# A list scheduler with new priorities: the same instructions of a decoder trunk, issued in another order

## The chip, the cores and the metric

The kernel runs on one core of one Trainium2 chip. The metric is device time in microseconds (us): the median of three runs of the kernel before is 1182.84 (1181.1 to 1184.08). Engines are named as in the profile: PE multiplies matrices, DVE, ACT and POOL do elementwise work, SP issues most DMAs.

## The reference, cut to what matters

Two decoder layers on one sequence of 512 rows with 1024 columns, all in float32:

```python
for l in range(DEPTH):                       # DEPTH = 2
    h = x @ w_in[l]
    q, k, v, u = jnp.split(h, splits, axis=-1)
    attn_out = diff_attention(q, k, v, lam, lam_init, subln_g[l], cos, sin)   # 4 heads, causal, rotary
    ssm_out = s5_ssm(u, ssm_lam_re[l], ...)  # 32 groups, complex diagonal scan, then GELU and GLU
    mix = jnp.concatenate([attn_out, ssm_out], axis=-1) @ w_out[l]
    x = layer_norm(ALPHA * x + mix, ln1_g[l], ln1_b[l])
    ff = jnp.square(jax.nn.relu(x @ w_ff1[l])) @ w_ff2[l]
    x = layer_norm(ALPHA * x + ff, ln2_g[l], ln2_b[l])
```

w_in maps 1024 to 2048 columns, w_ff1 1024 to 4096, w_ff2 back to 1024.

## The kernel before, in words

Each float32 product is made of three products of rounded parts. A weight block of 128x1024 comes by a DMA of SP's queue into a buffer `raw`; ACT rounds it to `whi`; the rest `wlo` = raw - whi is made by one of three routes, chosen by letters in the table `PLAN`: "V" a subtraction on DVE, "P" the same on POOL, "A" a negated rounding on ACT followed by an accumulating DMA from POOL's queue (`wsplit`, line 542, and `gsplit`). PE then runs hi by hi, hi by lo and lo by hi (`mm3`). There are five `raw` buffers and four each of `whi` and `wlo`.

A layer has these stages. The back stage makes q, k, v and u by projections, four heads of attention (`attn_u`, one unit for each head and block of 128 queries), the S5 part in four quarters (parameters `ssm_pars` and `ssm_outp`, then `ssm_a`, `ssm_b`, `ssm_c`) and the gated unit `glu`. Then come w_out with the first norm, and the feed-forward stage in eight chunks: in each, `ffone` makes four products of w_ff1, and `fftwo` seven products of sums of blocks (m1 to m7) of w_ff2. The last chunk (`ffend`) ends with the second norm. Three quarters of the second layer's S5 parameters are made while the first layer's feed-forward runs, stored to DRAM (`keep`, 12 tiles of 256 KB), and loaded again later.

Nothing is issued as it is written. `Rec.add` (line 215) records every operation with its tiles. `Rec.schedule` gives each a rank (the longest chain behind it), and `Rec.run` (line 350) goes through time with a duration for each operation (`Rec.cost`, line 261), takes the ready operation of highest rank plus offset on each engine, and so makes one fixed order for each engine. The offsets are set around parts of the program by `early(n, pe)`, `n` for all engines but PE and `pe` for PE. A tile could take a buffer only in the order in which tiles were written (`turn` at line 405). Where the plan expects PE to wait, `fill` puts in products of a zero tile `wz` (columns 256, into a bank that is overwritten later); they are allowed only between the exponentials of an attention unit and its product with v (`rec.spare`, in `attn_u`). 18 such products stand at the program's start.

All engine work is recorded under line 492 of the kernel before, where it is issued, and so the profile's groups are told apart by tile names: `ps_acc`, `ps_sc`, `ps_s` are banks of PSUM.

Of the kernel before, what the change touches and what calls it, by code (L numbers as in the profile page):

```python
# [19 lines left out]
P = 128  # L20
# [29 lines left out]
    "lo": ["AVAVVAAAAAAVAAAAAAAA", "AAAAAAAAAAAAAAAVAAVP"],  # L50
    "eng": {"rope": ["VVV", "VVV"], "tab": ["VVVVVV", "VVVVVV"], "cg": ["VVVV", "VVVV"], "ch": ["VVVV", "VVVV"], "sa": ["VV", "VP"], "sb": ["VVVVVV", "VVVVVV"]},
# [6 lines left out]
    "s5o": "p1 p0 o0 a0 b0 p2 a1 c0 o1 b1 a2 c1 b2 p3 a3 o2 c2 o3 b3 c3",  # L58
# [14 lines left out]
    "po": -6000,  # L73
    "m3": 4,
    "gap": [250, 500],
# [34 lines left out]
class View:  # L110
# [37 lines left out]

    def cells(self):
        m = 0  # L150
        for c in np.unique(self.idx // self.t.cell):
            m |= 1 << int(c)
# [12 lines left out]
class Op:  # L165
    __slots__ = ("eng", "name", "a", "k", "succ", "nd", "dur", "tail", "tiles", "new", "rank", "t0", "t1", "ready", "n",
                 "soft", "move", "table", "off", "port", "rows")


class Rec:  # L170
    def __init__(self, nc):
        self.real = {"PE": nc.tensor, "DVE": nc.vector, "ACT": nc.scalar, "POOL": nc.gpsimd, "DMA": nc.sync}
        self.ops, self.tiles, self.spares = [], {}, {}
        self.off = (0, 0)
# [86 lines left out]
    def cost(self, op, views):  # L261
# [88 lines left out]
    def run(self):  # L350
# [4 lines left out]
        turn, live, rel, wait = {}, {}, {}, {}  # L355
        for key, ts in self.tiles.items():
            turn[key], rel[key], wait[key] = 0, [0.0] * ts[0].bufs, []
            for i, t in enumerate(t for t in ts if t.first is not None):
                t.n = i
        left = {}  # L360
# [14 lines left out]
        for op, (a, b) in self.spares.items():  # L375
            for o in a:
                opens.setdefault(o, []).append(op)
            closes[b] = op
            op.nd, op.ready = len(a), 0.0
        while len(order) < len(self.ops):  # L380
# [23 lines left out]
            for v in op.new:  # L404
                if turn[v.key] != v.n or not rel[v.key]:
# [10 lines left out]
            for v in op.new:  # L416
                heapq.heappop(rel[v.key])
                turn[v.key] += 1
# [16 lines left out]
            if op in closes and closes[op] in live:  # L435
                live.remove(closes[op])
# [42 lines left out]
            for key in woken:  # L479
                for o in wait[key]:  # L480
                    heapq.heappush(future[o.eng], (max(o.ready, rel[key][0] if rel[key] else t), o.n, o))
# [14 lines left out]
def trunk(ctx, tc, x, xt, w_qk, w_v, w_u, w_glu, w_out, w_ff1, w_ff2, lam_qk, subln, lam_s, bc_s, d_s, glu_b,  # L496
# [40 lines left out]


# [89 lines left out]
    for i in range(PLAN["warm"]):  # L628
        PE.matmul(wb_[:, 0:256], wz[:, 0:P], wz, start=True, stop=True)
# [418 lines left out]
    def attn_u(l, h, b):  # L1048
# [13 lines left out]
        for m in range(2):  # L1062
            PE.matmul(scm[m][:, :n], qT[m][:, b * P:n], kT[m][:, :n], start=True, stop=False)
# [19 lines left out]
        for j in range(b + 1):  # L1083
            op = PE.matmul(o[:, 0:P], ats[:, j, :], vj(j), start=(j == 0), stop=(j == b))
            if j == 0:
                rec.spare(ex, op, o[:, 0:256], wz[:, 0:P], wz, start=True, stop=True)
# [201 lines left out]
    for l in range(L):  # L1288
# [6 lines left out]
        for h in range(NH):  # L1295
            t0 = PLAN["att"][l][h]
            for b in range(NB):
                side[min(t0 + b, len(back))].append(lambda h=h, b=b: attn_u(l, h, b))
            side[min(max(t0 + NB, PROJ * (h > 1)), len(back))].append(lambda h=h: attn_fin(l, h))
        s5 = []  # L1300
        made = [l > 0 and PLAN["store"][qd] in "sx" for qd in range(4)]
        def S(f, qd):
            return lambda: f(l, qd)
# [22 lines left out]
        for i in range(len(back) + 1):  # L1326
            if i < len(back):
                p0 = 0
                back[i]()
                d = 0  # L1330
            else:
                d = 0
            for fs, off, pe in ((side[i], PLAN["ao"][l], PLAN["ap"][l]), (s5side[i], PLAN["so"][l], PLAN["sp"][l])):
                with early(off, pe):
                    for f in fs:
                        f()

# [306 lines left out]
```

## Time and profile before

| what | us |
|---|---|
| median of three runs | 1182.84 |
| the profiled execution | 1184.34 |
| its span, first to last instruction | 1182.6 |
| PE busy in the span | 1124.1 (95%) |
| DVE busy | 883.4 (75%) |
| ACT busy | 643.7 (54%) |
| POOL busy | 382.9 (32%) |
| mean granted clock of PE | 0.987 of full speed |

The first layer runs from 0 to about 600 us, its back stage to about 200; the second layer's back stage lies between about 600 and 800. An instruction's duration on PE includes the way through the array; how fast PE goes is read from the distance of two starts. A clock of 1.00 is 2.4 GHz, 0.50 is 1.2 GHz.

### The profile page before, as it was taken

To read this page: it belongs to the slowest core of one execution; us is meant where nothing else is said; L and a number is where in the kernel's file an instruction comes from. 1 tells how busy PE (TensorE), PEld (TensorE's weight loads), DVE (VectorE), ACT (ScalarE), POOL (GpSimd) and SP (SyncE) were. 2 spreads that over 40 slices of the span, in tenths; PEclk is the share of its full clock that TensorE was granted. 3 is DMA by queue.
4 is the path that set the end of the run, shared out by engine and by line. 5 is a ranking of instruction groups with operands and counts; after the bars stand their busy time and mean duration, and the time that the engine had idled before them with its cause. 6 is when DMAs were issued, how large, how long until landed. Compare 5 with 4: busy or idle time off the path is not lost.

```text
span 1182.6 us, 16083 instructions
## 1 busy us (share of the span) xinstructions
PE 1124.1 (95%) x5755; PEld 933.8 (79%) x5755; DVE 883.4 (75%) x1517; ACT 643.7 (54%) x1214; POOL 382.9 (32%) x250
## 2 busy tenths in 40 slices
PE   8798989999999999999998989999999999999997
PEld 6678867788888888878888878777988787777775
DVE  7898997876867866878873978767587657656668
ACT  6677778425554555455256777763454445354450
POOL 1010111234454443553221211123344435445341
PEclk9899999999999999999999999999999999999999
DMA  7532624442653654565683663532553554464341
GB/s 242 150 80 72 150 74 134 149 128 73 175 144 93 168 149 109 168 166 133 204 212 89 174 174 94 176 108 85 155 153 98 165 144 114 133 161 117 114 125 72
DMA packets 52689, 160.41 MB, mean 136 GB/s; under 512 B 7041, under 2 KB 7297, under 8 KB 52609
## 3 DMA queue, kind: packets, MB, share of 16 engines
q1 hardware_dynamic: 42240, 121.63, 31.6%
q0 software_dynamic: 10368, 37.75, 17.1%
q8 instruction: 45, 0.74, 0.3%
q14 instruction: 36, 0.29, 0.1%
HBM read 110.07 MB, written 7.34 MB: 99 GB/s over the span
## 4 chain that ended last, share of the span: by engine, by line
PE 63%; ACT 12%; issue 7%; DMA 7%; DVE 6%; POOL 4%; SPq 1%; DVEq 0%; ACTq 0%; POOLq 0%
PE ps_acc L492 36%; PE ps_sc L492 15%; PE ps_s L492 12%; DMA wlo<-raw 6%; POOL wlo L492 4%; ACT whi L492 3%; ACT u L492 3%; DVE slot L492 2%; ACT xq L492 1%; ACT at L492 1%; DVE xq L492 1%; ACT wlo L492 1%; DMA raw<-in_w_qk_dram 1%; ACT slot L492 1%; SPq L492 1%
## 5 line engine op out<-in xcount | busy, mean ns | idle before, releaser
L492 POOL TENSOR_TENSOR wlo<-raw,whi 128x1024 fp32r<-128x1024 f32 x110 | 276.8, 2519 | 355.6 <-ACT whi L492 355.6
L492 ACT CAST whi<-raw 128x1024 fp32r<-128x1024 f32 x222 | 230.0, 1049 | 271.4 <-PE ps_acc L492 112.9
L492 PE MATMUL ps_acc<-xTh,whi 128*128 128x512 f32 (+1 forms) x712 | 269.3, 382 | 18.1 <-ACT whi L492 13.8
L492 PE MATMUL ps_acc<-xTh,wlo 128*128 128x512 f32 (+1 forms) x712 | 270.1, 383 | 6.7 <-DMA wlo<-raw 6.7
L492 PE MATMUL ps_acc<-xTl,whi 128*128 128x512 f32 (+1 forms) x712 | 268.3, 381 | 1.1 <-DVE xTl L492 1.0
L492 PE MATMUL ps_sc<-whi,slot 128*128 128x512 f32 x784 | 257.8, 393 | 1.6
L492 PEld LDWEIGHTS ps_sc<-whi,slot 128*128 128x128 f32 x784 | 147.1, 188 | 37.3 <-DVE xq L492 3.2
L492 PEld LDWEIGHTS ps_acc<-xTh,whi 128*128 128x128 f32 x712 | 135.1, 190 | 43.2 <-ACT whi L492 15.3
L492 PEld LDWEIGHTS ps_acc<-xTh,wlo 128*128 128x128 f32 x712 | 135.1, 190 | 34.1 <-DMA wlo<-raw 11.1
L492 PEld LDWEIGHTS ps_acc<-xTl,whi 128*128 128x128 f32 x712 | 135.4, 190 | 25.3 <-DVE xTl L492 2.3
L492 PE MATMUL ps_sc<-wlo,slot 128*128 128x512 f32 x392 | 152.7, 390 | 0.0
L492 POOL DMA_DIRECT2D wlo<-raw x72 | 63.3, 880 | 181.3 <-ACT wlo L492 141.1
L492 DVE TENSOR_TENSOR slot<-slot 128x512 fp32r<-128x512 f32 (+4 forms) x147 | 104.6, 733 | 18.9 <-ACT slot L492 17.5
L492 ACT ACTIVATE wlo<-raw 128x1024 fp32r<-128x1024 f32 x72 | 75.9, 1058 | 60.7 <-PE ps_s L492 32.8
L492 DVE TENSOR_TENSOR xq<-xq,ps_sc 128x512 f32<-128x512 f32 x124 | 84.1, 680 | 21.0 <-PE ps_sc L492 21.0
L492 DVE TENSOR_TENSOR raw<-raw 128x1024 f32<-128x1024 f32 x56 | 84.2, 1504 | 4.9 <-DMA raw<-in_w_ff_dram 3.1
L492 DVE TENSOR_TENSOR mh<-rt,ps_acc 128x512 f32<-128x512 f32 x28 | 19.3, 688 | 90.1 <-ACT rt L492 90.1
L492 PEld LDWEIGHTS ps_sc<-wlo,slot 128*128 128x128 f32 x392 | 73.6, 188 | 14.4
L492 PE MATMUL ps_acc<-whi,xTh 128*128 128x256 f32 (+1 forms) x176 | 57.4, 329 | 3.3 <-ACT u L492 2.0
L492 DVE TENSOR_TENSOR wlo<-raw,whi 128x1024 fp32r<-128x1024 f32 x40 | 48.7, 1221 | 11.3 <-ACT whi L492 10.2
L492 PE MATMUL ps_acc<-wlo,xTh 128*128 128x256 f32 (+1 forms) x176 | 56.5, 326 | 0.0
L492 PE MATMUL ps_acc<-whi,xTl 128*128 128x256 f32 (+1 forms) x176 | 56.3, 324 | 0.0
(228 smaller groups left out, 1942.9 us busy)
## 6 DMA issues: line engine op xcount, KB each, us to landing
raw<-in_w_ff_dram SPq DMA_DIRECT2D x128, 512.0 KB, 4.1
wlo<-raw POOLq DMA_DIRECT2D x72, 512.0 KB, 6.0
raw<-in_w_qk_dram SPq DMA_DIRECT2D x16, 512.0 KB, 4.5
raw<-in_w_out_dram SPq DMA_DIRECT2D x16, 512.0 KB, 4.1
raw<-in_w_u_dram SPq DMA_DIRECT2D x8, 512.0 KB, 4.4
raw<-in_w_v_dram SPq DMA_DIRECT2D x8, 512.0 KB, 7.1
rt<-rt SPq DMA_DIRECT2D x64, 64.0 KB, 2.0
at<-in_ln_dram SPq DMA_DIRECT2D x16, 256.0 KB, 4.6
```

Source lines behind the costliest of these rows:

```text
L492: getattr(self.real[op.eng], op.name)(*[_real(x) for x in op.a], **{n: _real(x) for n, x in op.k.items()})
```

## The change

The scheduler's rules change in four ways. A tile may take a free buffer when fewer earlier tiles than there are free buffers still wait for one (`todo` with `bisect` in place of `turn`). The durations of DMAs are other numbers. A table `pri` adds an offset for each named part (layer, then part: `1a30` is unit 0 of head 3 in layer 1, `0ssm_a1` quarter 1 of the S5 scan's first piece in layer 0), one for the engines but PE and one for PE. And one more `spare` allows zero products from the warm-up to the first attention product of layer 0. The rest are new values of `PLAN`: routes of the splits (`flo` for w_ff1 by block number modulo 4, `glo` for m1 to m7 of w_ff2, `nlo` for w_out, `elo` for the last chunk), offsets, and the written order of parts.

```diff
-        "u0 q0 k0 u1 u2 v0 v1 q1 k1 u3 v2 q2 k2 v3 q3 k3 g0 g1 g2 g3".split(),
+        "u0 k0 u2 q0 u1 v0 v1 q1 k1 u3 v2 q2 k2 v3 q3 k3 g0 g1 g2 g3".split(),
...
-    "att": [[8, 13, 13, 17], [8, 12, 15, 18]],
-    "s5": [[3, 15], [0, 14]],
+    "att": [[8, 11, 14, 18], [8, 12, 15, 18]],
+    "s5": [[4, 14], [3, 13]],
...
-    "flo": "APAV",
-    "nlo": "VPVPVPPV",
-    "glo": "PPPPPAP",
+    "flo": "AVVV",
+    "nlo": "APVAVPPV",
+    "glo": "VPPPAPV",
...
-    "elo": "VVPV",
+    "elo": "VVVV",
...
-    "ao": [-8000, -4000],
-    "so": [2000, 11000],
-    "ap": [24500, 40750],
-    "sp": [25000, 39000],
-    "pw": -4000,
+    "ao": [-6000, 4000],
+    "so": [2000, 19000],
+    "ap": [40500, 56750],
+    "sp": [31000, 27000],
+    "pw": -6000,
...
-    "po": -6000,
+    "po": 2000,
...
+        op.group = self.group
+        op.off += PLAN["pri"].get(op.group, (0, 0))[e == "PE"]
...
-            op.move = max(o.idx.size * (o.p[1] - o.p[0]) * 4 / 360.0, 180.0)
+            op.move = max(o.idx.size * (o.p[1] - o.p[0]) * 4 / 325.0, 180.0)
             if e != "DMA":
 
-                op.move *= 2
-            return (650.0 if o.p[1] - o.p[0] == 32 else 475.0) if e == "DMA" else 1030.0, 1550.0 + op.move
+                op.move *= 1.75
+            return (650.0 if o.p[1] - o.p[0] == 32 else 475.0) if e == "DMA" else 1030.0, 1550.0 + 1.35 * op.move
...
-                if turn[v.key] != v.n or not rel[v.key]:
+
+                if bisect.bisect_left(todo[v.key], v.n) >= len(rel[v.key]):
                     held = v.key
                     break
...
-                turn[v.key] += 1
+                todo[v.key].remove(v.n)
...
-                done = move + 900.0
+                done = move + 900.0 + 0.35 * op.move
...
-        PE.matmul(wb_[:, 0:256], wz[:, 0:P], wz, start=True, stop=True)
+        op = PE.matmul(wb_[:, 0:256], wz[:, 0:P], wz, start=True, stop=True)
+    heads = []
+    rec.spare([op], heads, wb_[:, 0:256], wz[:, 0:P], wz, start=True, stop=True)
...
+            if l == 0 and m == 0:
+                heads.append(op)
```

Two entries of the new table:

```python
"0ssm_a1": [18000, 8000], "1a21": [12000, -6000],
```

On ACT, this stood in the first layer after the casts that make the first weights (`whi` and `wlo` are the parts of a weight, `u` the S5 input copied out of a PSUM bank, `xq` parts of q and k); before:

```order
L492 COPY u<-ps_acc 32x128 x11
L492 CAST xq<-rt 64x512 x6
L492 COPY u<-ps_acc 32x128 x2
L492 COPY raw<-ps_acc 128x512
L492 COPY u<-ps_acc 32x128 x12
L492 ACTIVATE wlo<-raw 128x1024
L492 COPY u<-ps_acc 32x128 x2
L492 CAST whi<-raw 128x1024
L492 ACTIVATE wlo<-raw 128x1024
L492 CAST whi<-raw 128x1024
L492 ACT_TABLE_LOAD
```

And in the changed kernel, at the same place of ACT's program:

```order
L506 ACT_TABLE_LOAD
L506 ACTIVATE mh<-mh 128x32 x2
L506 CAST whi<-raw 128x1024 x2
L506 ACTIVATE rt<-ps_acc 128x512
L506 ACTIVATE wlo<-raw 128x1024
L506 CAST whi<-raw 128x1024
L506 COPY u<-ps_acc 32x128 x16
L506 CAST xq<-rt 64x512 x2
L506 ACTIVATE wlo<-raw 128x1024
L506 COPY u<-ps_acc 32x128 x16
L506 CAST whi<-raw 128x1024
```

Three rounded weights stand ahead of the first copies of `u`, and one behind the second 16, where two stood behind all 32 of the first two u blocks.

On SP's queue, at the end of the first layer's feed-forward (`keep` is a store of S5 parameters, `w_u`, `w_qk` and `w_v` are weights of the second layer); before:

```order
L492 DMA keep_4854<-xq 128x512 x2
L492 DMA raw<-in_w_ff_dram 128x1024
L492 DMA keep_4854<-xq 128x512
L492 DMA raw<-in_w_ff_dram 128x1024
L492 DMA keep_4854<-xq 128x512
L492 DMA raw<-in_w_ff_dram 128x1024 x5
L492 DMA keep_5214<-xq 128x512
L492 DMA raw<-in_w_ff_dram 128x1024 x2
L492 DMA keep_5214<-xq 128x512 x2
```

And in the changed kernel, from the last feed-forward weights on:

```order
L506 DMA raw<-in_w_ff_dram 128x1024 x56
L506 DMA raw<-in_w_u_dram 128x1024
L506 DMA raw<-in_w_qk_dram 128x1024
L506 DMA raw<-in_w_u_dram 128x1024
L506 DMA keep_5571<-xq 128x512 x4
L506 DMA raw<-in_w_qk_dram 128x1024
L506 DMA keep_5630<-xq 128x512 x3
L506 DMA slot<-keep_5571 128x512
L506 DMA raw<-in_w_u_dram 128x1024
L506 DMA keep_5688<-xq 128x512 x2
```

All twelve stores stand behind the last feed-forward weight now, among the first weights of the second layer; before, eight of them stood between feed-forward weights.

On POOL, in the second layer's feed-forward, a stretch that comes again for every two chunks; before:

```order
L492 DMA wlo<-raw 128x1024 x2
L492 TENSOR_TENSOR wlo<-raw,whi 128x1024 x2
L492 DMA wlo<-raw 128x1024
L492 TENSOR_TENSOR wlo<-raw,whi 128x1024 x5
L492 DMA wlo<-raw 128x1024 x2
L492 TENSOR_TENSOR wlo<-raw,whi 128x1024 x3
L492 DMA wlo<-raw 128x1024
L492 TENSOR_TENSOR wlo<-raw,whi 128x1024 x4
```

And in the changed kernel, in the same stage:

```order
L506 TENSOR_TENSOR wlo<-raw,whi 128x1024 x2
L506 DMA wlo<-raw 128x1024
L506 TENSOR_TENSOR wlo<-raw,whi 128x1024 x4
L506 DMA wlo<-raw 128x1024
L506 TENSOR_TENSOR wlo<-raw,whi 128x1024
L506 DMA wlo<-raw 128x1024
L506 TENSOR_TENSOR wlo<-raw,whi 128x1024
L506 DMA wlo<-raw 128x1024
```

For two chunks there are 8 subtractions and 4 DMAs in place of 14 and 6; the others went to DVE.

## Rows read from the trace of the kernel before

**Rows 1.** Busy time by stretch: from:to, length, then each engine's, clock, DMA share

```profile
0.00:20.00 20.00, 15.66 (x62) 11.75 (x63) 13.49 (x35) 12.87 (x21) 2.50 (x7) 0.91 0.92 326
40.00:60.00 20.00, 14.25 (x79) 11.83 (x78) 15.06 (x69) 16.35 (x46) 1.89 (x2) 0.83 0.47 107
160.00:200.00 40.00, 35.15 (x224) 27.64 (x224) 32.76 (x70) 31.15 (x87) 5.66 (x6) 0.96 0.32 106
200.00:600.00 400.00, 396.02 (x1881) 328.86 (x1881) 308.09 (x433) 193.96 (x295) 164.39 (x85) 1.00 0.51 142
600.00:620.00 20.00, 18.70 (x148) 17.77 (x147) 12.50 (x23) 13.70 (x25) 5.36 (x7) 1.00 0.96 230
600.00:800.00 200.00, 186.06 (x1160) 158.11 (x1158) 139.65 (x276) 142.47 (x351) 38.50 (x45) 0.98 0.56 147
800.00:1150.00 350.00, 342.86 (x1585) 281.35 (x1585) 235.67 (x298) 158.38 (x202) 150.82 (x78) 1.00 0.48 131
```

**Rows 2.** Waits of PE in the whole span: total us, times, longest

```profile
PE ps_acc L492 <- ACT whi L492: 13.8, 6, 4.5
PE ps_acc L492 <- DMA wlo<-raw: 6.7, 9, 1.8
```

**Rows 3.** Timeline of PE near the start: start, us, instruction

```profile
11.00 0.63 PE L492 MATMUL ps_acc<-xTh,wlo 128*128 128x512 f32 x1
11.43 0.63 PE L492 MATMUL ps_acc<-xTh,whi 128*128 128x512 f32 x1
```

**Rows 4.** The chain that ended last, two pieces: start, us, products

```profile
256.88 4.46 PE ps_acc L492 x35
280.30 5.47 PE ps_acc L492 x24
```

**Rows 5.** Timeline of PE from 47 us, with the idle time before

```profile
47.49 0.80 PE L492 MATMUL ps_acc<-xTh,whi 128*128 128x512 f32 x1 [4.50 <-ACT whi L492]
...
48.51 0.42 PE L492 MATMUL ps_acc<-whi,xTh 128*128 128x256 f32 x1
...
52.14 0.41 PE L492 MATMUL ps_acc<-whi,xTl 128*128 128x256 f32 x1
```

**Rows 6.** Timeline of ACT in the same stretch

```profile
41.53 3.21 ACT L492 COPY u<-ps_acc 32x128 f32<-32x128 f32 x12
44.77 1.06 ACT L492 ACTIVATE wlo<-raw 128x1024 fp32r<-128x1024 f32 x1
...
46.39 1.04 ACT L492 CAST whi<-raw 128x1024 fp32r<-128x1024 f32 x1
```

**Rows 7.** The zero products, by the tile wz: ns min/median/max, first and last start

```profile
L492 PE MATMUL ps_sc<-wz x83: 269/273/421, 1.4 to 704.0; 128*128 128x256 bf16 x83
```

**Rows 8.** Timeline of DVE, then of POOL, near 174 us

```profile
173.63 0.68 DVE L492 TENSOR_TENSOR xq<-rt,xq 64x512 fp32r<-64x512 f32 x1
...
174.87 2.73 DVE L492 TENSOR_TENSOR xq<-rt,xq 64x512 fp32r<-64x512 f32 x1
...
174.57 2.49 POOL L492 TENSOR_TENSOR wlo<-raw,whi 128x1024 fp32r<-128x1024 f32 x1
```

**Rows 9.** Groups by line: busy us, mean ns, idle before and its end

```profile
L492 POOL TENSOR_TENSOR wlo<-raw,whi 128x1024 fp32r<-128x1024 f32 x110 | 276.8, 2519 | 355.6 <-ACT whi L492 355.6
L492 DVE TENSOR_TENSOR wlo<-raw,whi 128x1024 fp32r<-128x1024 f32 x40 | 48.7, 1221 | 11.3 <-ACT whi L492 10.2 <-PE ps_acc L492 1.0
L492 DVE TENSOR_TENSOR slot<-mh,slot 128x512 fp32r<-128x512 f32 x32 | 39.9, 1247 | 5.2 <-ACT slot L492 4.1
L492 DVE TENSOR_TENSOR slot<-slot,ps_s 128x512 f32<-128x512 f32 x32 | 20.9, 682 | 16.2 <-PE ps_s L492 16.1
```

**Rows 10.** Timelines of ACT, POOL and PE at one wait for the accumulating DMA

```profile
1082.13 1.06 ACT L492 ACTIVATE wlo<-raw 128x1024 fp32r<-128x1024 f32 x1
...
1083.73 0.86 POOL L492 DMA_DIRECT2D wlo<-raw  x1 [2.15 <-ACT rt L492]
...
1089.04 0.50 PE L492 MATMUL ps_acc<-xTh,wlo 128*128 128x512 f32 x1 [1.84 <-DMA wlo<-raw]
```

**Rows 11.** DMA issues by line: KB each, median us to landing

```profile
wlo<-raw POOLq DMA_DIRECT2D x72, 512.0 KB, 6.0
```

More of the change, by code (lines that the diff above doesn't have):

```diff
@@ L1 @@
+import bisect
 import heapq
@@ L147, in real @@
         return r
+    seen = {}
     def cells(self):
-        m = 0
-        for c in np.unique(self.idx // self.t.cell):
-            m |= 1 << int(c)
+        z = (self.idx.astype(np.int32).tobytes(), self.t.cell)
+        m = self.seen.get(z)
+        if m is None:
+            m = 0
+            for c in np.unique(self.idx // self.t.cell):
+                m |= 1 << int(c)
+            self.seen[z] = m
         n, q = 0, self.t.prows
@@ L166 @@
     __slots__ = ("eng", "name", "a", "k", "succ", "nd", "dur", "tail", "tiles", "new", "rank", "t0", "t1", "ready", "n",
-                 "soft", "move", "table", "off", "port", "rows")
+                 "soft", "move", "table", "off", "port", "rows", "group")
 class Rec:
@@ L173, in __init__ @@
         self.ops, self.tiles, self.spares = [], {}, {}
-        self.off = (0, 0)
+        self.off, self.group = (0, 0), ""
     def pool(self, real, space):
@@ L354, in run @@
         ready = {e: [] for e in engs}
-        turn, live, rel, wait = {}, {}, {}, {}
+        todo, rel, wait = {}, {}, {}
         for key, ts in self.tiles.items():
-            turn[key], rel[key], wait[key] = 0, [0.0] * ts[0].bufs, []
+            todo[key], rel[key], wait[key] = [], [0.0] * ts[0].bufs, []
             for i, t in enumerate(t for t in ts if t.first is not None):
                 t.n = i
+                todo[key].append(i)
         left = {}
@@ L377, in run @@
                 opens.setdefault(o, []).append(op)
-            closes[b] = op
+            for o in b:
+                closes.setdefault(o, []).append(op)
             op.nd, op.ready = len(a), 0.0
@@ L434, in run @@
                 busy[1] += over
-            if op in closes and closes[op] in live:
-                live.remove(closes[op])
+            for z in closes.get(op, ()):
+                if z in live:
+                    live.remove(z)
             op.t0, op.t1 = t, t + op.dur
@@ L536, in early, with named @@
         rec.off = old
+    def named(g, f, *a):
+        rec.group = g
+        f(*a)
     def lo_mode(l, n):
@@ L1062, in attn_u @@
         for m in range(2):
-            PE.matmul(scm[m][:, :n], qT[m][:, b * P:n], kT[m][:, :n], start=True, stop=False)
+            op = PE.matmul(scm[m][:, :n], qT[m][:, b * P:n], kT[m][:, :n], start=True, stop=False)
+            if l == 0 and m == 0:
+                heads.append(op)
             PE.matmul(scm[m][:, :n], qT[m][:, b * P:n], kT[2 + m][:, :n], start=False, stop=False)
@@ L1085, in attn_u @@
             if j == 0:
-                rec.spare(ex, op, o[:, 0:256], wz[:, 0:P], wz, start=True, stop=True)
+                rec.spare(ex, [op], o[:, 0:256], wz[:, 0:P], wz, start=True, stop=True)
         A.copy(on[:, b, :], o[:, 0:P])
@@ L1297, in trunk @@
             for b in range(NB):
-                side[min(t0 + b, len(back))].append(lambda h=h, b=b: attn_u(l, h, b))
-            side[min(max(t0 + NB, PROJ * (h > 1)), len(back))].append(lambda h=h: attn_fin(l, h))
+                side[min(t0 + b, len(back))].append(lambda h=h, b=b: named(f"{l}a{h}{b}", attn_u, l, h, b))
+            side[min(max(t0 + NB, PROJ * (h > 1)), len(back))].append(lambda h=h: named(f"{l}e{h}", attn_fin, l, h))
         s5 = []
@@ L1328, in trunk @@
                 p0 = 0
+                rec.group = f"{l}{PLAN['back'][l][i]}"
                 back[i]()
+                rec.group = ""
                 d = 0
@@ L1336, in trunk @@
                         f()
+                        rec.group = ""
         xbs, sts_ = {}, {}
```

11 lines of the change are left out of this document (6 added, 5 removed).

## The prediction

> **What bounds the kernel now.** I read the busy time by stretch first, then PE's waits, then timelines around the longest of them. PE is busy 396.02 of 400 us between 200 and 600 and 342.86 of 350 between 800 and 1150 [rows 1]: in w_out and the feed-forward stages PE is the bound, and a schedule can give back about 11 us there at most. The back stages are looser: 14.25 of 20 us between 40 and 60, 35.15 of 40 between 160 and 200, 186.06 of 200 in the second layer's [rows 1]. In the first layer's back stage DVE has hardly a pause and PE waits for what comes out of DVE and ACT; the second layer's has 139.65 of 200 us of DVE and 142.47 of ACT, so it is bound by chains and not by one engine [rows 1]. By cause PE's longest waits are 13.8 us for ACT's rounded weights and 6.7 us for the accumulating DMA that finishes `wlo` [rows 2]. The change moves no arithmetic of PE: it adds 85 zero products (the 83 that stand, 273 ns each through the array [rows 7], become 168) and reorders. So the question is which idle time and which slow-clock time goes away, and what fills it.
>
> **Head.** Near 11 us products of 512 columns start 0.43 us apart [rows 3]; later 24 such take 5.47, or 0.228 each [rows 4]. The clock is at 1.2 GHz there after PE idled 3 us behind its warm-up products. The change puts 30 zero products ahead of the first product in place of 18, and 11 more behind the first and sixth. If the clock holds at 2.4 GHz, about 8 products gain 0.2 each, 1.6 us. A zero product has no row of its step; the nearest, 35 products mostly of 256 columns in 4.46 us [rows 4], gives 0.127 each, so the 11 behind the first cost up to 1.4 if PE would not have waited. Bounds -1.6 to +1.4; I take -0.5, because the data that arrive may set the pace anyhow.
>
> **The wait at 43 to 47 us.** PE idles 4.50 us for `whi`, the longest wait of the program [rows 5]. ACT is not slow there, it is in the wrong order: the rounding at 46.39 stands behind 12 copies of `u` that take 3.21 and a `wlo` of 1.06 [rows 6]. Behind the wait the clock is at half: 17 steps from 48.51 to 52.14 are 0.214 each [rows 5] where 0.127 was had [rows 4], 1.5 us more. The new ACT order has three roundings ahead of the first 16 copies, so both should go, 6.0 us; the plan puts 12 zero products near this place, a wait of 12 x 0.127 = 1.5 that it still expects. Bounds 0 (the wait only moves to the `u` copies, which are now late for the S5 part) to -6.0; I take -4.5.
>
> **The end of the first layer's back stage.** Here 54 zero products stood and 115 stand now, so the plan expects 61 x 0.127 = 7.7 us more waiting in this place, and as much less before it. DVE's work up to the fourth `glu` is the same but for one sum of each S5 quarter, which `PLAN` moves to POOL: four operations of 128x512, 0.68 each by the nearest row [rows 9], 2.7 us. PE's idle time of 160 to 200 is 4.85 us [rows 1]. One subtraction on DVE took 2.73 us there instead of 0.68, because POOL's 2.49 us subtraction had begun 0.3 us earlier [rows 8]. Bounds: +7.7 (the 61 stand where PE has work) to -11.7 (the idle 4.85 and the 54 x 0.127 of zero products both go). I take -3, nearest to the DVE work that goes.
>
> **Feed-forward.** The routes move: of w_ff1's 64 blocks the accumulating DMA keeps 16 in place of 32; in all it goes from 72 to 60, POOL's subtractions from 110 to 62 and DVE's from 40 to 100. The DMA route is slow: ACT's part ends at 1083.19, POOL issues at 1083.73, and PE goes on at 1089.04 after 1.84 of waiting [rows 10]; 6.0 us is the median to landing [rows 11], against 1.221 on DVE [rows 9]. All nine of PE's waits for it sum to 6.7 [rows 2]. Half of w_ff1's such blocks go, which is 3.4; I take -3.5, bounds -6.7 to the price below. What it costs is on DVE: 62 more subtractions in these stages (two fewer in w_out) at 1.221 are 75.7 us. DVE has 308.09 + 235.67 = 543.8 of 750 us there [rows 1], so it comes to 619, 83%; PE covers it as long as no split is late. DVE is also held up less: its 128x512 subtraction of two SBUF tiles takes 1.247 on average and one of the same size that reads PSUM 0.682 [rows 9], 0.565 a piece, and 48 POOL subtractions go away.
>
> The row at 174.87 ends 0.54 after POOL's, as if DVE had not begun before [rows 8]. The Trainium skill (SBUF — State Buffer, "SBUF: two separate sides") says that DVE and GpSimd share a port pair as an exclusive lock for a whole instruction; the trace agrees. That rule speaks for fewer POOL subtractions and against more DVE ones of two SBUF inputs, each of which can now be the one that is locked out; by it a newly moved split can be late by up to 2.73 - 0.68 = 2.05 us. It is weighed below as a rival.
>
> **The second layer's back stage.** PE idles 13.9 us of 200 [rows 1]. Priorities for nearly each attention unit change, and weights are issued ahead of reloads. Against it stand the 8 `keep` stores that moved to the layer boundary: 8 x 256 KB are 2.1 MB, at the 230 GB/s of the stretch whose DMA share is already 0.96 [rows 1] 9.1 us more of DMA, with the second layer's fourth and fifth weights behind them in SP's queue. They are off PE's path if the stretch after 620 has room. Bounds +9.1 to -13.9; I take -4, since most of the boundary's weights stand ahead of the stores.
>
> **Sum.** -0.5 - 4.5 - 3 - 3.5 - 4 = -15.5. The profiled execution took 1184.34, so 1168.8; it was 1.5 above the median of the runs, which gives **1167** on that scale. The last products' tail and the 1.4 us ahead of PE's first instruction stay.
>
> **The rivals.** *Bound by DVE, the gains given back* (0.15): in the first layer DVE's sum is unchanged, so what PE saves at 43 us turns into the zero products at the end, and boundary DMAs take the second layer's gain. Of the sum only the head, the DVE sums and half of the feed-forward term stay: -0.5 - 2.7 - 1.7 = -5, or 1178. For it speaks that the plan itself lists 7.7 us more waiting; against, that DVE too sat idle in the stretch from 40 to 60 (15.06 of 20) [rows 1], so that wait was not DVE's.
> *More than half of the waits go* (0.15): all of the 6.0 at 43 us, 5 of the feed-forward's 6.7, 8 of the second layer's 13.9 and 11.7 at the back stage's end, with the head's 1.6: -32, or 1150. For it: PE's waits have many small causes, which priorities reach; against: chains of the S5 part are no shorter.
> *Splits late on DVE* (0.12): 60 splits moved to DVE in the stage where PE has no slack. Each waits in DVE's order behind operations that POOL locks out, 0.565 on average and 2.05 at worst. If PE waits for all of them at the average it costs 34 us; with the other four terms at -12.0 the time is 1182.8 - 12.0 + 34 = 1205, and the kernel is slower from 12.0 / 0.565 = 22 late splits on. With 35 late it is 1191, which I give as its time. Against it: DVE would be 83% busy, and `whi` and `wlo` have four buffers, so a split has some three products of 5.47 us [rows 4] to be made.
> *Zero products and reordering miss* (0.10): durations in the plan are not the chip's, the 85 zero products stand where PE has work, 85 x 0.127 = 10.8, and take back the two gains of the first layer and part of the third: about 1182, no change.
>
> **How the numbers follow.** The forecast has 0.48, with a range of its own of 1159 to 1176. A measurement here can tell about 0.3%, 3.5 us, from no change. Faster: 0.48 + 0.15 + 0.15 and a little of the others, 0.78. Same: most of the misses, 0.09. Slower: the late splits and a rest, 0.13. The range must take in 1150 and reach to the slow side until 2 in 10 are left out: 1150 to 1186.
>
> **What would show it.** Right: ACT's roundings ahead of the copies of `u` and no PE wait over 3 us between 20 and 60; a clock of 1.00 in the stretches 0 to 20 (0.91 before) and 40 to 60 (0.83) but for the start; PE's waits for the accumulating DMA under 4 us; PE idle in the second layer's back stage under 11 us. DVE's mean for the 128x512 subtraction of two SBUF tiles should fall below 1.247. Wrong: PE waits for DVE `wlo` in the feed-forward stages; PE waits for weights of the second layer with DMA share near 1; zero products in a stretch in which PE had no idle time and which is longer by their number. If PE's busy time grows by about as much as its idle time falls, the zero products only renamed the waits.

## The result, and the profile after

| | before | after |
|---|---|---|
| median, us (range) | 1183.46 (1181.1 to 1184.27) | 1151.41 (1150.47 to 1152.2) |
| span of the profiled execution, us | 1182.6 | 1149.7 |
| PE busy in the span, us | 1124.1 | 1117.1 |
| mean granted clock of PE | 0.987 | 0.997 |

The ratio is 0.9732, with a 95% interval of 0.9715 to 0.9749: the changed kernel is about 32 us faster, twice what was forecast. It lies outside the 1159 to 1176 that the forecast had for itself and just inside the whole range of 1150 to 1186. The first part of its page, busy time by engine:

```profile
PE 1117.1 (97%) x5840; PEld 936.0 (81%) x5840; DVE 912.5 (79%) x1569; ACT 632.2 (55%) x1202; POOL 260.3 (23%) x198
```

PE does 85 instructions more and is busy 7.0 us less, so the zero products have not merely renamed waits. Its idle time fell from 58.5 to 32.6 us, and part of that fall is still only covered: in the run without zero products, below, PE idles 42.0 us. The stretches of the program lie up to 33 us earlier than before; these are the windows of after that answer to [rows 1], in the same columns:

```profile
0.00:20.00 20.00, 18.54 (x93) 14.40 (x94) 13.43 (x44) 14.02 (x23) 2.50 (x7) 1.00 0.92 329
40.00:60.00 20.00, 18.98 (x115) 15.93 (x114) 18.09 (x78) 14.78 (x41) 1.72 (x2) 1.00 0.22 50
160.00:180.00 20.00, 17.75 (x133) 14.97 (x132) 17.47 (x40) 10.44 (x34) 0.42 (x2) 0.94 0.24 70
200.00:570.00 370.00, 367.68 (x1755) 307.66 (x1754) 290.19 (x400) 176.79 (x259) 99.87 (x55) 1.00 0.46 131
570.00:590.00 20.00, 19.35 (x85) 15.53 (x85) 18.64 (x36) 2.28 (x5) 2.00 (x2) 1.00 0.58 191
570.00:770.00 200.00, 192.83 (x1207) 165.86 (x1207) 156.00 (x312) 143.88 (x350) 38.53 (x47) 1.00 0.62 164
770.00:1120.00 350.00, 348.12 (x1639) 290.19 (x1638) 266.72 (x337) 158.22 (x206) 90.60 (x49) 1.00 0.45 124
```

The clock column is full from 0 to 20 and from 40 to 60, where it was 0.91 and 0.83 (in both kernels the first zero products, up to 5.2 us, still start 0.213 us apart and later ones 0.109, so the column does not show the half speed at the very start), and PE's pauses in the feed-forward stages are 2.3 of 370 and 1.9 of 350 us. Of PE's waits in the whole span, the first four of after:

```profile
PE ps_acc L506 <- ACT u L506: 4.4, 5, 1.6
PE ps_s L506 <- ACT mx L506: 2.8, 2, 1.6
PE ps_sc L506 <- ACT at L506: 2.5, 6, 0.8
PE ps_s L506 <- ACT idw L506: 2.1, 3, 1.3
```

Both waits of [rows 2] are gone from this list, the 13.8 us for `whi` and the 6.7 for the accumulating DMA; what is left is small and has many causes. ACT's order near the wait of [rows 6] is now this (start, duration, operation):

```profile
23.75 1.06 ACT L506 ACTIVATE wlo<-raw 128x1024 fp32r<-128x1024 f32 x1
24.72 1.03 ACT L506 CAST whi<-raw 128x1024 fp32r<-128x1024 f32 x1
25.66 4.27 ACT L506 COPY u<-ps_acc 32x128 f32<-32x128 f32 x16
...
32.52 4.28 ACT L506 COPY u<-ps_acc 32x128 f32<-32x128 f32 x16 [0.22 <-PE ps_acc L506]
36.82 1.05 ACT L506 CAST whi<-raw 128x1024 fp32r<-128x1024 f32 x1
```

The roundings stand ahead of the copies of `u`, as the prediction said. The groups that answer to [rows 9], DVE's first, then POOL's:

```profile
L506 DVE TENSOR_TENSOR wlo<-raw,whi 128x1024 fp32r<-128x1024 f32 x100 | 122.0, 1221 | 47.1 <-ACT whi L506 47.0
L506 DVE TENSOR_TENSOR slot<-mh,slot 128x512 fp32r<-128x512 f32 x32 | 21.8, 688 | 0.0
L506 DVE TENSOR_TENSOR slot<-slot,ps_s 128x512 f32<-128x512 f32 x32 | 20.7, 683 | 22.0 <-PE ps_s L506 21.8
L506 POOL TENSOR_TENSOR wlo<-raw,whi 128x1024 fp32r<-128x1024 f32 x62 | 156.2, 2519 | 418.7 <-ACT whi L506 410.9
```

The subtraction of two SBUF tiles, 1247 ns on average before, takes 688, no longer than the one that reads PSUM (683). The accumulating DMAs (count, size, median us to landing) and the zero products (ns min/median/max, first and last start), for [rows 11] and [rows 7]:

```profile
wlo<-raw POOLq DMA_DIRECT2D x60, 512.0 KB, 5.3
```

```profile
L506 PE MATMUL ps_sc<-wz x168: 272/273/421, 1.4 to 182.0; 128*128 128x256 bf16 x168
```

**Where the time went.** Both kernels run the same real products in a slightly different order. I added up their durations at full clock (without zero products) as they come in each trace, and noted when PE had done so much of this work. The table is after minus before at equal work; before reaches these points at 38.0, 79.3, 145.3, 221.8, 558.6, 641.6, 833.0 and 1146.2 us.

| work done, us | 25 | 50 | 100 | 150 | 475 | 550 | 700 | 1000 |
|---|---|---|---|---|---|---|---|---|
| after, us | -2.0 | -12.0 | -14.3 | -6.0 | -12.3 | -8.3 | -22.4 | -32.8 |

So 12 us are won by 50 us of work; 8 of 14 are given back at the end of the first layer's back stage (100 to 150); w_out and the first feed-forward bring 6.3; the layer boundary takes 4.0; the second layer's back stage brings 14.1, and what follows 10.4. Since the order differs slightly, the entries at 550 move by up to 2 us with the duration that is assumed for a product, and those at 475 by up to 1; the last one does not move.

**The clock has a part in it.** (1 - 0.987) x 1182.6 is 15.4 us of PE's time lost to the half clock before, (1 - 0.997) x 1149.7 is 3.4 after, so at most 12 of the 32.9 us are clock. A short wait of before shows how it was lost; PE near the accumulating DMA of [rows 10]:

```profile
1090.30 0.39 PE L492 MATMUL ps_acc<-xTl,whi 128*128 128x512 f32 x1
1090.53 0.59 PE L492 MATMUL ps_acc<-xTh,wlo 128*128 128x512 f32 x1
1090.92 0.63 PE L492 MATMUL ps_acc<-xTh,whi 128*128 128x512 f32 x1
1091.35 0.63 PE L492 MATMUL ps_acc<-xTl,whi 128*128 128x512 f32 x1
...
1093.90 0.43 PE L492 MATMUL ps_acc<-xTl,whi 128*128 128x512 f32 x1
```

PE had waited 1.84 us and was busy again from 1089.04; 1.5 us later its products start 0.43 apart in place of 0.23, at 1.2 GHz, until 1093.9. The wait of 1.84 cost another 1.6. Not every wait has this behind it: PE waited 1.98 us until 74.58, and the clock from 60 to 80 is 1.00. In the second layer's back stage of before the window from 695 to 720 had a clock of 0.86:

```profile
695.00:720.00 25.00, 22.17 (x119) 17.68 (x118) 17.86 (x40) 15.99 (x39) 4.64 (x7) 0.86 0.40 100
```

That is another 3.5 us. Idle time alone, from which the prediction took its bounds, leaves both out.

It leaves out a third part. Weight loads (PEld) can wait while PE is still counted as busy with the product before; the next products then only start farther apart. In the kernel before they waited 11.1 us for the accumulating DMA, where PE's own idle time for it was 6.7 [rows 2]:

```profile
PEld ps_acc L492 <- DMA wlo<-raw: 11.1, 12, 2.3
```

By the distances of starts, the 10.4 us won from 700 to 1000 of work are about 4.8 of idle time, 1.7 of half clock and 3.9 inside busy time.

### The profile page after: what moved, and what is told of

Its sections match the earlier page's. It is cut to its first block, busy times and chain, and to the rows that moved or that the text cites. A ratio compares the mean times of both kernels' runs of the same rounds, so it can differ in the third digit from the quotient of the medians.

```text
span 1149.7 us, 16190 instructions
## 1 busy us (share of the span) xinstructions
PE 1117.1 (97%) x5840; PEld 936.0 (81%) x5840; DVE 912.5 (79%) x1569; ACT 632.2 (55%) x1202; POOL 260.3 (23%) x198
## 3 DMA queue, kind: packets, MB, share of 16 engines
q1 hardware_dynamic: 42240, 121.63, 32.6%
## 4 chain that ended last, share of the span: by engine, by line
PE 66%; ACT 5%; DVE 2%; issue 2%; DMA 1%; SPq 0%; DVEq 0%; ACTq 0%; POOLq 0%
PE ps_acc L506 35%; PE ps_sc L506 23%; PE ps_s L506 8%; ACT whi L506 1%; ACT u L506 1%; DVE xq L506 1%; DVE wlo L506 1%; ACT at L506 1%; ACT wlo L506 1%; DMA wlo<-raw 0%; DMA keep<-xq 0%; ACT xq L506 0%; ACT xTh L506 0%; DVE xTl L506 0%; DMA xq<-xs 0%
## 5 line engine op out<-in xcount | busy, mean ns | idle before, releaser
L506 PE MATMUL ps_sc<-whi,slot 128*128 128x512 f32 x784 | 254.5, 391 | 1.2 <-DVE xq L506 0.6
L506 POOL TENSOR_TENSOR wlo<-raw,whi 128x1024 fp32r<-128x1024 f32 x62 | 156.2, 2519 | 418.7 <-ACT whi L506 410.9
L506 DVE TENSOR_TENSOR wlo<-raw,whi 128x1024 fp32r<-128x1024 f32 x100 | 122.0, 1221 | 47.1 <-ACT whi L506 47.0
L506 DVE TENSOR_TENSOR slot<-slot 128x512 fp32r<-128x512 f32 (+4 forms) x143 | 126.5, 893 | 6.5 <-ACT slot L506 6.0
L506 POOL DMA_DIRECT2D wlo<-raw x60 | 53.0, 887 | 231.5 <-ACT wlo L506 114.6
L506 ACT ACTIVATE wlo<-raw 128x1024 fp32r<-128x1024 f32 x60 | 63.4, 1059 | 61.9 <-PE ps_s L506 32.4
L506 DVE TENSOR_TENSOR raw<-raw 128x1024 f32<-128x1024 f32 x56 | 68.4, 1221 | 0.6
L506 ACT CAST slot<-slot 128x512 fp32r<-128x512 f32 x56 | 34.5, 617 | 51.1 <-DVE slot L506 49.1
```

What stands on the lines that cost most here:

```text
L506: getattr(self.real[op.eng], op.name)(*[_real(x) for x in op.a], **{n: _real(x) for n, x in op.k.items()})
```

## The experiments

The diffs are against the kernel that each heading names. For each run the table below gives its time at equal work against the profile of before, as above. Each run had runs of the kernel before beside it on the same chip; ratios are to those. Differences in us below are of medians from different chips, on which the kernel before has medians of 1181.63 to 1184.28; taken by the ratios they come out up to 1.3 us otherwise, so a difference under 2 us is not told from none.

| run | zero products | 50 | 150 | 475 | 550 | 700 | 1000 | median us |
|---|---|---|---|---|---|---|---|---|
| after | 168 | -12.0 | -6.0 | -12.3 | -8.3 | -22.4 | -32.8 | 1151.41 |
| routes alone | 103 | 0.0 | -1.3 | +1.8 | +4.7 | +6.2 | -1.9 | 1181.65 |
| old routes | 174 | -11.8 | -3.6 | -6.2 | -4.4 | -16.1 | -22.6 | 1162.07 |
| rules alone | 169 | -4.6 | +1.4 | -1.6 | +1.7 | -6.0 | -12.6 | 1174.55 |
| no priorities | 123 | -8.4 | -3.9 | -11.2 | -7.5 | -16.1 | -26.4 | 1158.56 |
| old DMA durations | 131 | -9.1 | -2.8 | -9.7 | -8.2 | -16.6 | -27.0 | 1157.83 |
| buffers in turn | 249 | +6.8 | +9.3 | +12.5 | +20.0 | +25.2 | +19.6 | 1203.34 |
| no zero products | 18 | -10.3 | -5.4 | -11.7 | -8.8 | -21.9 | -32.3 | 1152.0 |
| less DVE | 168 | -12.3 | -6.9 | -13.2 | -9.6 | -23.9 | -34.3 | 1150.3 |
| short operands | 168 | -11.4 | -9.5 | -15.8 | -12.3 | -26.3 | -36.6 | 1147.38 |
| stores early | 168 | -11.5 | -5.5 | -11.8 | -3.7 | -18.0 | -28.4 | 1155.61 |
| mx shared | 168 | -12.1 | -10.4 | -16.7 | -13.0 | -27.4 | -37.7 | 1146.89 |

**The routes of the weight splits, alone and taken out.** The kernel before with the four new route strings; then the changed kernel with the four old ones.

```diff
-    "flo": "APAV",
-    "nlo": "VPVPVPPV",
-    "glo": "PPPPPAP",
+    "flo": "AVVV",
+    "nlo": "APVAVPPV",
+    "glo": "VPPPAPV",
...
-    "elo": "VVPV",
+    "elo": "VVVV",
```

> The kernel before with the four new route strings (flo, nlo, glo, elo) and nothing else of the change. Theory A (the routes of the splits are what the feed-forward stages gained by, since PE's waits for the accumulating DMA, 4.2 us in the second layer's alone, are gone in the changed kernel): 10 us in the second layer's feed-forward and 3 to 6 in the first, so 1168 to 1172. Theory B (the routes only pay with the new DMA durations, which place POOL's issues): 1178 to 1186.

> The changed kernel with the four old route strings. Theory A (routes): the second layer's feed-forward gets its 10 us back and the first's some 3, so 1163 to 1166. Theory B (the rules of the scheduler place even the old routes well): 1151 to 1156.

Alone: 1181.65, ratio 0.9993 (0.9981 to 1.0006), no change. Taken out of the changed kernel: 1162.07, ratio 0.983 (0.9815 to 0.9845), so there they are worth 10.7 us. With the routes alone the second feed-forward does gain 8.1 us (700 to 1000), but the new plan puts 20 S5 parameter products together in the first feed-forward (407.6 to 412.6 us; in the kernel before 4 stand there). PE there, with its idle time:

```profile
410.96 2.08 PE L492 MATMUL ps_s<-idw,gx 128*128 128x144 f32 x12 [2.18 <-ACT idw L492]
414.24 0.80 PE L492 MATMUL ps_sc<-whi,slot 128*128 128x512 f32 x1 [1.20 <-ACT slot L492]
416.33 1.22 PE L492 MATMUL ps_sc<-whi,slot 128*128 128x512 f32 x2 [0.86 <-DVE slot L492]
```

Three waits and the half clock behind them (0.77 from 404 to 426) take back what the routes gave there, and another 4.4 us are lost between 475 and 700. The time is in theory B's range. A route's worth depends on the plan around it.

Taken out, the time lies near theory A's range, but not for its reason. Only 3.7 us come back in the first feed-forward and 3.9 in the second, not 3 and 10, and PE's waits for the accumulating DMA do not come back with the old routes. First the run with the old routes, then the rules alone (next section), which has the old routes too:

```profile
PE ps_s L506 <- DMA wlo<-raw: 0.5, 1, 0.5
```

```profile
PE ps_s L506 <- DMA wlo<-raw: 0.6, 1, 0.6
```

With the new routes in the old plan 1.9 us are left, of 6.7 before. So the new rules take these waits away by themselves, and the routes most of them. What the old routes do cost in the new plan is seen at the weight loads of the second feed-forward, which then wait 4.8 us for DVE's `xq`, and not for it with the new routes; and at DVE's subtraction of two SBUF tiles, in the run with the routes alone and then with the old routes:

```profile
L492 DVE TENSOR_TENSOR slot<-mh,slot 128x512 fp32r<-128x512 f32 x32 | 21.1, 685 | 1.4 <-ACT slot L492 1.4
L506 DVE TENSOR_TENSOR slot<-mh,slot 128x512 fp32r<-128x512 f32 x32 | 43.6, 1371 | 1.1 <-ACT slot L506 1.0
```

**The rules alone, and the priorities taken out.** The new scheduler with the old `PLAN`; the changed kernel with an empty `pri`.

```diff
-    "pri": {"1a30": [-2000, -16000], "1q1": [12000, 18000], ...
+    "pri": {},
```

> The changed scheduler (buffers out of turn, new DMA durations, zero products at the head) with the table PLAN of before and no entry in pri. Theory C (the rules carry the back stages): the second layer's back stage keeps most of its 14.4 us and the time is 1163 to 1170. Theory D (the priorities carry them): under 5 us in all, 1178 to 1184.

> The changed kernel with an empty table pri. Theory D (the priorities carry the second layer's back stage): 10 to 14 us of the 14.4 come back there, 1161 to 1167 or more. Theory C (the rules carry it): 1151 to 1156.

Rules alone: 1174.55, ratio 0.994 (0.9923 to 0.9956), between the two theories. Without priorities: 1158.56, ratio 0.9797 (0.9781 to 0.9813), so they are worth 7.1 us, again between the two theories, most of it in the second layer's back stage: from 550 to 700 of work 14.1 us are won with them and 8.6 without.

**The DMA durations and the buffers out of turn, each put back.**

```diff
-            op.move = max(o.idx.size * (o.p[1] - o.p[0]) * 4 / 325.0, 180.0)
+            op.move = max(o.idx.size * (o.p[1] - o.p[0]) * 4 / 360.0, 180.0)
...
-                op.move *= 1.75
-            return (650.0 if o.p[1] - o.p[0] == 32 else 475.0) if e == "DMA" else 1030.0, 1550.0 + 1.35 * op.move
+                op.move *= 2
+            return (650.0 if o.p[1] - o.p[0] == 32 else 475.0) if e == "DMA" else 1030.0, 1550.0 + op.move
...
-                done = move + 900.0 + 0.35 * op.move
+                done = move + 900.0
```

```diff
-                if bisect.bisect_left(todo[v.key], v.n) >= len(rel[v.key]):
+                if todo[v.key][0] != v.n or not rel[v.key]:
```

> The changed kernel planned with the DMA durations of before. Theory E (the durations are the part of the rules that works: with the old ones the plan thinks that weights and reloads land earlier than they do): PE's waits for DMAs and for the accumulating DMA come back, 6 to 9 us, 1157 to 1161. Theory F (buffers out of turn are the part that works): 1151 to 1155.

> The changed kernel with tiles that take buffers only in the order in which they are written, as before. Theory F (buffers out of turn work): 6 us or more come back, most in the second layer's back stage, 1157 to 1165. Theory E (the DMA durations work): 1151 to 1155.

Old durations: 1157.83, ratio 0.9792 (0.9775 to 0.981), 6.4 us slower than the changed kernel. That is in theory E's range, but PE's waits for the accumulating DMA, which E gave as the reason, come back only to 0.5 us; its longest waits are for ACT's `u` (6.1), ACT's `mx` (3.5) and DVE's `slot` (2.9). Buffers in turn: 1203.34, ratio 1.0175 (1.0152 to 1.0198), 52 us slower than the changed kernel and slower than before, far outside both expectations. The new table needs the freedom: under the old rule its plan is worse than the kernel before. That PE waits there for what stands behind a buffer's turn was not followed up to a buffer. The first waits of PE in that run:

```profile
PE ps_sc L506 <- ACT at L506: 7.3, 14, 1.3
PE ps_acc L506 <- ACT u L506: 5.6, 4, 2.0
PE ps_sc L506 <- ACT xq L506: 4.4, 6, 1.8
PE ps_acc L506 <- DMA wlo<-raw: 4.3, 4, 1.9
```

The parts do not add up: 7.6 for the rules alone and 0 for the routes alone, but 10.7, 7.1, 6.4 and 52 when one is taken out of the whole of 32.

**No zero products.** The changed kernel with all other instructions in the same order; only the 18 of the warm-up are kept.

```diff
-        order += extra
```

> The changed kernel in exactly its own order, with all zero products but the 18 of the warm-up left out of the instruction stream. Theory G (they only stand where PE waits and hold the clock): the clock falls to half at the head and between 140 and 180 us, for some 7 to 14 us in all, which costs 2 to 5 us: 1153 to 1157. Theory H (the end of the first layer's back stage hangs on DVE and ACT, so that PE's clock there costs nothing, and the zero products cost nothing either): 1150 to 1153, and only the head's 1.6 us show.

1152.0, ratio 0.9748 (0.9733 to 0.9762), in theory H's range. 150 zero products bring 0.6 us by the medians and 1.9 by the ratios, whose intervals overlap, and cost nothing that shows. Without them the profile shows the waits that they had covered, and the clock that they had held. Stretches of this run, then the first of PE's waits between 145 and 200 (total us, times, longest):

```profile
150.00:160.00 10.00, 6.06 (x28) 4.79 (x26) 9.91 (x24) 7.12 (x19) 0.31 (x1) 0.67 0.60 183
160.00:180.00 20.00, 12.87 (x66) 9.75 (x65) 18.07 (x42) 11.26 (x37) 1.39 (x2) 0.76 0.21 66
```

```profile
PE ps_sc L505 <- DVE at L505: 8.4, 3, 4.7
```

The clock is at 0.67 and 0.76 there, against 0.94 with zero products, and the end is where it was: PE had nothing to do that the others waited for. The longest of these waits are for `at`, a part of the attention, from DVE.

**Is DVE the bound at the end of the first layer's back stage?** DVE is busy 9.91 of 10 us from 150 to 160 in the run above. The changed kernel in its own order, with the 24 DVE operations of the first layer's rotary embedding on 8 columns in place of 512.

```diff
+        n0 = len(rec.ops)
...
+        if l == 0:
+            for op in rec.ops[n0:]:
+                op.a = tuple(x[:, 0:8] for x in op.a)
```

> The changed kernel in exactly its own order; the three rotary operations on DVE for each q and k of the first layer (24 operations) run on 8 columns in place of 512, so the rotation of the first layer is left out and some 24 x 0.53 = 12.7 us of DVE work go. Theory I (DVE bounds the first layer's back stage, where PE was 14 us ahead after 100 us of its work and gave 8 of them back by 125): the time falls by 5 to 8, 1143 to 1146. Theory J (the stage hangs on the chain through PE and ACT): under 2, 1149 to 1152.

1150.3, ratio 0.9732 (0.9716 to 0.9749): DVE is busy 84.58 us in place of 90.57 between 100 and 200, and the time falls by 1.1 by the medians and by nothing by the ratios, as theory J said. So this DVE work is not what bounds the stage, though DVE has hardly a gap; it is spread over the time that another chain takes. DVE's work on the attention, for which PE waits in the run above, was not shortened in any run.

**Which chain?** In the changed kernel's timelines PE waits twice for `mx`, and ACT makes `mx` and `hx` one behind the other. PE first, then ACT:

```profile
158.19 0.49 PE L506 MATMUL ps_s<-mx,u 128*128 128x128 f32 x2 [1.63 <-ACT mx L506]
...
167.99 5.51 PE L506 MATMUL ps_sc<-wz 128*128 128x256 bf16 x49
...
176.80 0.49 PE L506 MATMUL ps_s<-mx,u 128*128 128x128 f32 x2 [1.19 <-ACT mx L506]
```

```profile
156.01 2.13 ACT L506 COPY mx<-m 128x128 f32<-128x128 f32 x7
158.16 1.66 ACT L506 COPY hx<-slot 64x256 f32<-64x256 f32 x4
...
174.60 2.14 ACT L506 COPY mx<-m 128x128 f32<-128x128 f32 x7
```

One run shortens this chain by leaving out work:

```diff
+        n0 = len(rec.ops)
...
+        if l == 0:
+            for op in rec.ops[n0:]:
+                op.a = tuple(x[:, 0:1] if isinstance(x, View) else x for x in op.a)
+                op.k = {n: x[:, 0:1] if isinstance(x, View) else x for n, x in op.k.items()}
```

> The changed kernel with every instruction of every engine in the same order, only that the operands of the S5 products of the first layer (the seven copies to mx, the four DVE products and sums and the four copies to hx of each of its four channel quarters) are made for one of four channel blocks; the other three are left as they are, so three quarters of these operands are left out. Theory J (the end of the first layer's back stage follows one chain, DVE parameters, then ACT's mx and hx copies, then the products of that quarter): in the profile of the changed kernel the 7 mx copies take 2.13 us and the 4 hx copies 1.66 us, and PE waits 1.63 and 1.19 us for mx; at a third of their length some 2.5 us of ACT per quarter go and, with the DVE products, up to 4 us per quarter; with two of the four quarters on the path the time is 1144 to 1148. Theory K (the chain that ends there is another: the attention's softmax on ACT and DVE, or the products themselves): 1149 to 1152.

1147.38, ratio 0.9699 (0.9675 to 0.9723): 4.0 us less, as theory J said, and nearly all of it between 100 and 150 of work. It shortens DVE's work of this part as well as ACT's. The next two keep the whole computation and take ACT's copies off the chain, which the idle POOL can share.

```diff
+        if l == 0:
+            c = [o for o in rec.ops[n0:] if o.eng == "ACT"]
+            edits[c[2]] = ["copy", (mx[0:64, :, 32:64], m3[64:128])]
+            edits[c[3]] = ["drop"]
+            for o in c[4:7]:
+                edits[o] = ["pool"]
...
```

> The changed kernel in its own order, the whole computation kept; in the first layer alone the seven ACT copies that fill mx become three on ACT (two of the 32-partition ones in one of 64 partitions) and three on POOL, which stands idle there for 9.98 and 9.54 us. Theory J (the copies to mx stand on the chain that ends the first layer's back stage, as the run with short operands says): the three on ACT take some 0.9 us in place of 2.13, PE's waits for mx, 1.63 and 1.19 us, shrink by up to 1.2 us each, the time is 1149 to 1150.5. Rival N (POOL's copies land later than ACT's did, or hold up DVE, so that the wait is for POOL instead): 1151 to 1154.

> As the run before, and two of the four copies to hx of each quarter of the first layer are on POOL too. Theory J: PE waits 0.38 and 0.36 us for hx after it waited for mx, so another 0.5 us or so, 1148.5 to 1150. Rival N: a 64x256 copy on POOL takes over twice ACT's 0.41 us, and PE waits for hx from POOL: 1151 to 1155.

With `mx` shared: 1146.89 (1146.62 to 1147.24), ratio 0.9695 (0.9672 to 0.9717), the fastest kernel of all, 4.5 us below the changed one and more than expected. The stretch from 50 to 150 of work gives back 1.7 us in place of 6.0. With `hx` shared too: 1147.2, ratio 0.9699 (0.9676 to 0.9722), the same. The copies of the first of these on both engines, by the tile `mx` (ns min/median/max, first and last start):

```profile
L506 POOL COPY mx<-m x9: 285/324/686, 96.8 to 171.7; 32x128 f32<-32x128 f32 x9
L506 ACT COPY mx<-m x9: 287/296/300, 101.0 to 171.7; 128x128 f32<-128x128 f32 x3, 32x128 f32<-32x128 f32 x3, 64x128 f32<-64x128 f32 x3
```

And PE's waits for these operands from 80 to 200, where the changed kernel had 2.8 us for `mx`:

```profile
PE ps_s L506 <- ACT hx L506: 0.7, 2, 0.4
PE ps_s L506 <- POOL mx L506: 0.5, 1, 0.5
```

The waits shrink by 2.3 us and the time by 4.5. The rest is probably ACT's queue: 1.5 us are there at 100 of work already, ahead of both waits, and whatever stands behind the copies on ACT can start earlier; no run separates this. Theory N is out: POOL's copy takes 324 ns in the median, near ACT's 296, and a 64x256 copy to `hx` in the last run 396 on POOL against 404 on ACT. With `hx` on POOL, PE's waits for it are 0.8 us in place of 0.7, so nothing more was to be had.

**The layer boundary.** The changed kernel with `po` early again.

```diff
-    "po": 2000,
+    "po": -6000,
```

> The changed kernel with one number of its table put back: the weight of the second layer's S5 parameters and their stores is early again (po -6000 in place of 2000), the plan made anew from it. Theory L (the 4 us that the changed kernel lost between the first layer's feed-forward and the second layer's back stage are the parameter products that now stand there): PE at that place is 3 to 5 us ahead, the time 1146 to 1149. Theory M (they only change places: made earlier they take the same time from the first layer's feed-forward, whose products wait for them there): 1150 to 1158.

1155.61, ratio 0.9767 (0.9745 to 0.979), 4.2 us slower, and all of it at the boundary (475 to 550). The time is in theory M's range, but it tells neither theory from the other, because the parameter products did not move: 44 of the 128 start at 555 us or later, as in the changed kernel. What changed is the order of the stores and what stands around them. PE with its idle time, in the changed kernel and then in this run:

```profile
567.83 1.82 PE L506 MATMUL ps_s<-idw,gx 128*128 128x144 f32 x12 [1.30 <-ACT idw L506]
570.64 0.50 PE L506 MATMUL ps_s<-whi,slot 128*128 128x512 f32 x1 [0.53 <-DVE ks L506]
```

```profile
568.82 1.82 PE L506 MATMUL ps_s<-idw,gx 128*128 128x144 f32 x12 [1.35 <-ACT idw L506]
572.32 0.76 PE L506 MATMUL ps_s<-idw,gx 128*128 128x144 f32 x4 [1.68 <-DVE ks L506]
574.75 0.71 PE L506 MATMUL ps_s<-whi,slot 128*128 128x512 f32 x1 [1.67 <-ACT xq L506]
```

The waits grow from 1.8 to 4.7 us, and the clock from 556 to 600 is 0.96 in place of 1.00, another 1.7. What gathers these products at the boundary is, in part, the new routes: 18 start at 555 or later in the kernel before, 22 in the changed kernel with the old routes and 24 with the rules alone, against 44 in the changed kernel. But their number does not seem to set the loss from 475 to 550: it is 1.8 with 22, 3.3 with 24, and 1.5 with the old DMA durations, which have 42 there. What does stays open.

## Why the prediction was right in direction and half in size

| term | predicted | measured at equal work |
|---|---|---|
| head (0 to 25) | -0.5 | -2.0 |
| wait at 43 to 47 us (25 to 50) | -4.5 | -10.0 |
| end of the first layer's back stage (50 to 150) | -3 | +6.0 |
| feed-forward (150 to 475, 700 to 1000) | -3.5 | -6.3 and -10.4 |
| boundary and second layer's back stage (475 to 700) | -4 | +4.0 and -14.1 |
| sum | -15.5 | -32.8 |

The spans differ by 32.9, so the table is complete.

**Head: right mechanism.** The clock is full in 0 to 20, and the early products run at it. "I take -0.5, because the data that arrive may set the pace anyhow" was too careful at first. But the run without zero products has the head at -0.3 at 25 of work and -11.7 at 475, 0.6 from the changed kernel: a head start of 1.7 us shrank to 0.6 in what follows.

**The wait at 43 us and the end of the back stage: the first larger, the second of the wrong sign.** The wait and its clock, 6.0 us together, went, and the same stretch gave 4 us more, from smaller waits. The claim that failed is "In the first layer's back stage DVE has hardly a pause and PE waits for what comes out of DVE and ACT", from which -3 was taken "nearest to the DVE work that goes". Less DVE brought 1.1 at most, sharing ACT's copies 4.5. A chain through ACT's copies ends last; PE arrives earlier and waits longer, so 8 of 14 us are given back. The rival "gains given back" had this mechanism and blamed the wrong engine. The plan's 61 more zero products had said so: 7.7 us of waiting by their number, bounded in the text as +7.7, and +8.3 came from 100 to 150. (A zero product starts 0.109 us after the last at full clock, not 0.127 as was taken from mixed products, so the 61 are 6.7.)

**Feed-forward: the term that was most too small, and its mechanism was another.** PE's waits for the accumulating DMA, 6.7 us, are off the list, as forecast, but the routes are not needed for it: alone they leave 1.9, the rules alone leave 0.6, and the new plan with the old routes 0.5. The -3.5 was taken from these waits, of which the routes had almost none left to win beside the rules. What they bring there lies elsewhere: within the new plan the old routes win 2.6 us from 150 to 475 and 6.5 from 700 to 1000, where the new ones win 6.3 and 10.4, so the routes' part is 7.6 in both layers, with DVE's two-SBUF subtraction at 688 ns in place of 1371. That this shorter DVE work is the whole of it is likely, and not shown by a run of its own. The prediction had this price, "0.565 a piece", and put no time to it. The rest, 9.1, is of the kind that the rules bring alone (3.0 and 6.6 in these stretches), and the prediction gave them nothing here. "A schedule can give back about 11 us there at most" is refuted by 16.7: it counted idle time only, and left out the half clock, 1.6 at 1090, and the weight loads' waits inside PE's busy time.

**Second layer's back stage: right direction, size outside the bound.** "PE idles 13.9 us of 200" made -13.9 the limit; -14.1 came, since 3.5 us of half clock stood beside the idle time; PE still idles 7.2 us of 200 there. Priorities bring some 5 of it, DMA durations about 6 and the rules alone 7.7 (+1.7 to -6.0); they overlap. The boundary cost 4.0 of the 9.1 allowed. That the stores cost it through the DMA is not shown: the DMA share is 0.58 from 570 to 590, and 1.8 us are PE's waits for `idw` and `ks` at the parameter products that now stand there. The rest stays open.

**The late splits did not come.** PE's only wait for a DVE `wlo` in the whole span is 0.4 us, and DVE's two-SBUF subtraction fell to 688 ns. In the kernel before, each of its 20 slow ones (over 0.8 us) overlaps a subtraction on POOL; in the changed kernel none of the 32 does, and none is slow. The Trainium skill (SBUF — State Buffer, "SBUF: two separate sides"), by which the shared ports are an exclusive lock, agrees with that. The fall comes with the routes (685 with them alone, 1371 without them in the new plan). The lock could still have hit the moved splits: with the routes alone DVE's `wlo` takes 1344 ns on average and 3079 at worst, in the new plan 1227 at worst. The moved splits are 73.3 us of DVE's time, and DVE is busy only 29.1 longer, at 77% in these stages and not the 83% forecast. What spoke against moving splits to DVE was weighed rightly as the smaller effect.

**"Zero products only renamed waits": neither good nor harm.** PE's busy time fell, so that test came out against it for the change as a whole. The zero products themselves do stand in waits: without them PE idles 42.0 us in place of 32.6, and the time is the same within 2 us.

The rival that came true is "more than half of the waits go", at 1150. Its pieces were 6.0, 5, 8, 11.7 and 1.6; the total is right, in part by luck: the 11.7 at the back stage's end did not come, and more than forecast elsewhere made up for it.

## What to carry to other kernels

A wait of PE costs more than its idle time when the clock falls behind it, so bounds taken from idle time are too narrow: add the slow stretch from the windows' clock column and look at what the weight loads wait for. That a wait is gone does not show which part of a change took it away; put one part back and look for it. An engine that is busy with hardly a gap need not be the bound; shorten its work with the order held fixed before believing it, and then shorten the chain, here small copies in ACT's queue, three of seven moved to POOL and two made one, worth 4.5 us. The parts of a schedule are worth what the rest of it makes of them: the same routes brought 0 alone and 10.7 inside.

## What was not expected of the hardware

Half clock came 1.5 us after PE was busy again, behind a wait of 1.84 us, and then lasted 3.4 us; behind a wait of 1.98 us at 74.58 there was none. In the run without zero products 17 us of half clock between 153 and 181 cost nothing that could be told from the noise. With 60 more splits on DVE, its other work became some 44 us shorter, of which four sums that went to POOL are 2.7. POOL's copy of 32x128 took 324 ns in the median, against 296 for ACT's of 32, 64 and 128 partitions, where a POOL subtraction of 128x1024 takes 2519 against DVE's 1221.
